# A temperature softmax whose middle loads and stores are joined in pairs

## The chip, the cores and the metric

The kernel runs on one core of a Trainium2 chip. The core has five engines with a program each: TensorE (PE), VectorE (DVE), ScalarE (ACT), GpSimd (POOL) and SyncE (SP). Data moves between the main memory (HBM) and the on-chip memory (SBUF, 128 partitions) by 16 DMA engines; SP, ACT and POOL ask for transfers, each through a queue of its own. The metric is the device time of one execution in microseconds (us). The kernel before takes 159.9 us, the median of 3 runs (159.85 to 159.92).

## The reference

The input is 16 x 1024 rows of 512 float32 numbers, 33.55 MB; the output is as large. Each row goes through a softmax at temperature 2:

```python
x_scaled = x / 2.0
x_max = np.max(x_scaled, axis=-1, keepdims=True)
exp_x = np.exp(x_scaled - x_max)
return exp_x / np.sum(exp_x, axis=-1, keepdims=True)
```

## The kernel before

The 16384 rows are spread over 128 partitions, 128 rows for each. Every partition's 128 rows are cut into ten tiles, in the order of the work: tile 0 with 3 rows, tile 1 with 5, and tiles 2 to 9 with 15 each (`TILES`, line 10; the second number is the tile's place). A row is 2048 bytes, so a 15-row tile is 30720 bytes on each partition, contiguous in HBM and in SBUF, and 3840 KB in all. The tiles lie in one SBUF tensor, `arena`, with room for 98 rows per partition: tiles 0 to 7 fill it, tile 8 lies again where tiles 0 to 2 were, and tile 9 over the rest of tile 2 and a part of tile 3.

The work of a tile is done in place:

- Its load: SP asks for tile 0, ACT for tile 1 (in three pieces, `SPREAD`) and then for tiles 2 to 7, all at the start (`early`, `loads`, line 119). POOL asks for tiles 8 and 9 later (line 177): `TURN` (83) makes it wait until the first 83 rows per partition are exponentiated, and `LATE` says which tiles' stores must have landed first (0, 1, 2 for tile 8; 3 for tile 9).
- ACT takes exp(x / 2) row by row with the row's sum into `stats` (lines 204 and 271), in chunks of 5 rows after the first 3. No maximum is subtracted; a check at the end sees to inputs for which that would not do.
- DVE takes the reciprocals of up to 15 sums (line 166) and multiplies up to 15 rows by them (line 169). For the last tile it does so in three steps of 5 rows.
- SP stores the tile once its multiplications are done (line 137), in the order of the tiles.

PE has a bookkeeping part: it waits for each tile's landing and adds the tile's number of chunks to a semaphore, from which ACT takes one for each chunk (line 194). At the end the sums are counted that lie between `LO` and `HI` (lines 180 to 196). If all do, the program ends when all stores have landed (lines 256 and 257); otherwise a second form of the computation, with the maximum, runs from line 239. In the profiled execution that second form doesn't run.

Each engine works through its own list in order; the three queues of transfers share the 16 DMA engines. A transfer over 128 partitions gives each DMA engine 8 of them, and the records of the profile have one packet per contiguous run, here one for each partition of a tile.

Of the kernel before, what the change touches and what calls it, by code (L numbers as in the profile page):

```python
# [10 lines left out]
    (3, 0), (5, 3), (15, 8), (15, 23), (15, 38), (15, 53), (15, 68), (15, 83), (15, 0), (15, 15),  # L11
]

LATE = {8: (0, 1, 2), 9: (3,)}
ARENA = 98

HEAD = [3]
# [2 lines left out]
SPREAD = 1  # L20
# [8 lines left out]
def kernel(  # L29
# [5 lines left out]
    nc = tc.nc  # L35
# [6 lines left out]
    xf = x.flatten_outer_dims()  # L42
    of = out.flatten_outer_dims()
# [16 lines left out]
    tiles, base = [], 0  # L60
# [2 lines left out]
        tiles.append((base, r, at))  # L63
        base += r

    def dram(ap, t):
        b, r, _ = tiles[t]
        return ap[b * P : (b + r) * P].rearrange("(p r) d -> p r d", r=r)

    def sb(t):  # L70
        _, r, at = tiles[t]
        return arena[:, at : at + r, :]

    straight = sum(HEAD)
# [3 lines left out]
    owner = [max(t for t, (b, _, _) in enumerate(tiles) if b <= s) for s in starts]  # L78
# [9 lines left out]
            pairs.append([k])  # L88
    upto = [1 + max(j for j, ks in enumerate(pairs) if owner[ks[0]] == t) for t in range(len(tiles))]

    ld = [nc.alloc_semaphore(f"ld{t}") for t in range(len(tiles))]
    s_home = {t: nc.alloc_semaphore(f"s_home{t}") for t in LATE}
    s_near = nc.alloc_semaphore("s_near")
    s_end = nc.alloc_semaphore("s_end")
    s_exp = nc.alloc_semaphore("s_exp")
    s_go = nc.alloc_semaphore("s_go")
    s_rec = nc.alloc_semaphore("s_rec")
    s_mul = nc.alloc_semaphore("s_mul")
# [11 lines left out]
    g_rec = nc.alloc_semaphore("g_rec")  # L110
    g_mul = nc.alloc_semaphore("g_mul")

    def load(eng, t):
        r = tiles[t][1]
        parts = [(0, P, 0, r)]
        if t == SPREAD:
            parts = [(0, P, 0, r - 1), (0, 126, r - 1, r), (126, P, r - 1, r)]
        for p, q, lo, hi in parts:
            eng.dma_start(  # L119
                out=sb(t)[p:q, lo:hi], in_=dram(xf, t)[p:q, lo:hi]  # L120
            ).then_inc(ld[t], 16)

    stored_by = {u: s_home[t] for t, us in LATE.items() for u in us}
    for t, (_, r, at) in enumerate(tiles):
        over = {u for u, (_, ru, au) in enumerate(tiles[:t]) if at < au + ru and au < at + r}
        assert over <= {u for v, us in LATE.items() if v <= t for u in us}

    def landings(ts):
        return 16 * len(list(ts))

    near = len(tiles) - 2
    sem_of = {**stored_by, near: s_near}
    at_end = landings(t for t in range(len(tiles)) if t not in sem_of)

    def store(eng, t):
        eng.wait_ge(s_mul, upto[t])
        eng.dma_start(out=dram(of, t), in_=sb(t)).then_inc(sem_of.get(t, s_end), 16)

    def take(eng, sem, n):
        eng.wait_ge(sem, n).then_inc(sem, -n)  # L140

    def rounds(eng, body):


        i = eng.alloc_register("general")
        eng.wait_ge(s_near, 16)
        eng.wait_ge(s_flag, 1)
        eng.reg_load(i, flag[0:1, 0:1])
        with eng.While(lambda: eng.snap(i, min_val=0, max_val=1) < 1):
            body()  # L150
            eng.reg_add(i, i, 1)

    def early():
        load(nc.sync, 0)
        load(nc.scalar, 1)

    def loads():
        for t in range(2, min(LATE)):
            load(nc.scalar, t)

    def program():

        for j, ks in enumerate(pairs):
            b, c = starts[ks[0]], sum(sizes[k] for k in ks)
            a = b % ARENA
            nc.vector.reciprocal(  # L166
                out=recip[:, b : b + c], in_=stats[:, b : b + c]
            )._wait_ge(s_exp, ks[-1] + 1).then_inc(s_rec, 1)
            nc.vector.tensor_mul(  # L169
                out=arena[:, a : a + c],  # L170
                in0=arena[:, a : a + c],
                in1=recip[:, b : b + c].unsqueeze(2).to_broadcast([P, c, D]),
            )._wait_ge(s_rec, j + 1).then_inc(s_mul, 1)

        nc.gpsimd.memset(ones[:, :], 1.0).then_inc(s_ones, 1)  # L175
        nc.gpsimd.wait_ge(s_exp, starts.index(TURN))
        for t, us in LATE.items():
            nc.gpsimd.wait_ge(s_home[t], landings(us))
            load(nc.gpsimd, t)
        nc.gpsimd.tensor_scalar(  # L180
            out=inside[:, :], in0=stats[:, :], scalar1=LO, scalar2=HI,
            op0=Alu.max, op1=Alu.min,
        )._wait_ge(s_exp, len(sizes)).then_inc(s_cnt, 1)
        nc.vector.scalar_tensor_tensor(  # L184
            out=inside[:, :], in0=inside[:, :], scalar=1.0, in1=stats[:, :],
            op0=Alu.mult, op1=Alu.is_equal, accum_out=count[:, :],
        )._wait_ge(s_cnt, 1).then_inc(s_cnt, 1)
        nc.vector.tensor_scalar(  # L188
            out=flag[:, :], in0=total[:, :], scalar1=float(N), scalar2=None, op0=Alu.is_ge,
        )._wait_ge(s_tot, 1).then_inc(s_flag, 1)  # L190


        for t in range(len(tiles)):
            nc.tensor.wait_ge(ld[t], 48 if t == SPREAD else 16).then_inc(s_go, owner.count(t))
        nc.tensor.wait_ge(s_ones, 1)
        nc.tensor.matmul(  # L196
            total[:, :], lhsT=count[:, :], rhs=ones[:, :], start=True, stop=True
        )._wait_ge(s_cnt, 2).then_inc(s_tot, 1)

        nc.scalar.preload_act_table(Exp)  # L200
        for k, c in enumerate(HEAD):
            take(nc.scalar, s_go, 1)
            for b in range(starts[k], starts[k] + c):
                ins = nc.scalar.activation(  # L204
                    out=arena[:, b], in_=arena[:, b], func=Exp, scale=0.5,
                    accum_out=stats[:, b : b + 1],
                )
            ins.then_inc(s_exp, 1)
        exponentials(straight, n_rows)

        for t in range(len(tiles)):
            store(nc.sync, t)

        x_g = xf.rearrange("(t p r) d -> t p r d", p=P, r=G)
        o_g = of.rearrange("(t p r) d -> t p r d", p=P, r=G)
        data = arena[:, 0:G]

        def vector():  # L220
            for i in range(n_rows // G):
                nc.vector.reduce_max(
                    out=g_max[:, :], in_=data, axis=mybir.AxisListType.X, negate=True
                )._wait_ge(g_go, i + 1).then_inc(g_top, 1)
                nc.vector.reduce_sum(
                    out=g_sum[:, :], in_=data, axis=mybir.AxisListType.X
                )._wait_ge(g_exp, i + 1).then_inc(g_add, 1)
                nc.vector.reciprocal(
                    out=g_sum[:, :], in_=g_sum[:, :]
                )._wait_ge(g_add, i + 1).then_inc(g_rec, 1)  # L230

        def scalar():
            for i in range(n_rows // G):
                nc.scalar.activation(out=data, in_=data, func=Exp, scale=0.5)._wait_ge(
                    g_sub, i + 1
                ).then_inc(g_exp, 1)

        def gpsimd():
            nc.gpsimd.wait_ge(s_end, at_end)
            for i in range(n_rows // G):  # L240
                nc.gpsimd.dma_start(out=data, in_=x_g[i]).then_inc(g_ld, 16)
                nc.gpsimd.wait_ge(g_ld, 16 * (i + 1)).then_inc(g_go, 1)
                nc.gpsimd.tensor_add(
                    out=data, in0=data, in1=g_max[:, :].unsqueeze(2).to_broadcast([P, G, D])
                )._wait_ge(g_top, i + 1).then_inc(g_sub, 1)
                nc.gpsimd.tensor_mul(
                    out=data, in0=data, in1=g_sum[:, :].unsqueeze(2).to_broadcast([P, G, D])
                )._wait_ge(g_rec, i + 1).then_inc(g_mul, 1)
                nc.gpsimd.wait_ge(g_mul, i + 1)
                nc.gpsimd.dma_start(out=o_g[i], in_=data).then_inc(g_st, 16)  # L250
                nc.gpsimd.wait_ge(g_st, 16 * (i + 1))

        rounds(nc.vector, vector)
        rounds(nc.scalar, scalar)
        rounds(nc.gpsimd, gpsimd)
        nc.sync.wait_ge(s_near, 16)
        nc.sync.wait_ge(s_end, at_end)
# [27 lines left out]
    at = next(k for k, i in enumerate(head) if type(i).__name__ == "InstDrain")  # L285
    entry.instructions = head[:at] + first + head[at:]
    act = []
    entry.instructions = list(entry.instructions) + [i for i in jumps if i not in act]
    nc.switch_body(here, parent=None, valid_engines=[i.engine for i in jumps])
    loads()  # L290
    program()


# [28 lines left out]
```

## Time and profile before

| What | Value |
|---|---|
| median of 3 runs | 159.9 us (159.85 to 159.92) |
| span of the profiled execution, first to last instruction | 158.7 us |
| difference between median and span, outside the span | 1.2 us |
| busy: ACT, DVE, POOL, PE | 80.8, 73.2, 2.2, 0.2 us |
| moved | 67.11 MB at 423 GB/s |
| packets | 3024, of which 336 under 512 bytes |
| ACT's first instruction of tiles 2, 3, 4, 5, 6, 7, 8, 9 | 17.71, 29.26, 41.77, 59.92, 78.08, 98.51, 112.74, 131.24 us |
| last store issued | 143.66 us |

The page gives no time of the profiled execution other than its span, so the span is set against the median. The slices of the page divide the span in 40 parts of 4 us each; a digit is a share in tenths. In the rows of the queues, the share is the time that a queue's packets took, of 16 engines' time in the span or in the stretch that was asked for. A queue name followed by q (SPq, ACTq) in the waits is the engine's instruction list itself. Numbers behind a transfer's row are its count, its size and the median time from its issue to its landing.

### The profile page before, as it was taken

The page shows a single profiled execution, that of the slowest core. Times are in us where ns is not written, and L with a number is a line of the kernel's source. Part 1 is how long each engine was busy: PE and PEld are TensorE (multiplying, and loading weights), DVE is VectorE, ACT ScalarE, POOL GpSimd, SP SyncE. Part 2 cuts the span into 40 slices and gives each one's busy share as a digit, 9 for nine tenths or more (in the row PEclk, how much of TensorE's full clock was granted, in tenths as well). Part 3 has the DMA queues.
Part 4 walks back from the last instruction along what each step waited for, and adds up shares of the span by engine and source line. Part 5 has one row for each costly group of instructions (what it writes and reads, how often), then busy time and mean ns, then how long its engine had stood idle before and what let it go on. Part 6 is the DMA issues. An engine that isn't in the chain of part 4 may idle for free. (4 is left out here: it accounts for less than half of the span.)

```text
span 158.7 us, 657 instructions
## 1 busy us (share of the span) xinstructions
PE 0.2 (0%) x2; PEld 0.1 (0%) x2; DVE 73.2 (46%) x27; ACT 80.8 (51%) x257; POOL 2.2 (1%) x8
## 2 busy tenths in 40 slices
PE   0000000000000000000000000000000000000000
PEld 0000000000000000000000000000000000000000
DVE  0047001992981990059500991008932981992000
ACT  0590598697498008940399001991597009940000
POOL 0000000000000000000000300000000000010000
DMA  7999998989999999999999999999999999999995
GB/s 271 382 496 396 463 437 324 480 382 485 410 457 410 457 410 449 418 449 418 441 426 441 426 434 434 426 441 426 441 418 449 418 449 410 457 403 465 403 457 256
DMA packets 3024, 67.11 MB, mean 423 GB/s; under 512 B 336, under 2 KB 336, under 8 KB 720
## 3 DMA queue, kind: packets, MB, share of 16 engines
q1 hardware_dynamic: 1584, 34.34, 50.4%
q10 hardware_dynamic: 1152, 24.90, 37.1%
q0 software_dynamic: 288, 7.86, 11.5%
HBM read 33.55 MB, written 33.55 MB: 423 GB/s over the span
## 5 line engine op out<-in xcount | busy, mean ns | idle before, releaser
L271 ACT ACTIVATE arena<-arena x125 | 76.8, 615 | 54.1 <-ACTq L140 54.1
L169 DVE TENSOR_TENSOR arena<-arena,recip 128x7680 f32<-128x7680 f32 (+2 forms) x12 | 70.2, 5847 | 0.4
L166 DVE RECIPROCAL recip<-stats 128x15 f32<-128x15 f32 (+2 forms) x12 | 2.7, 224 | 70.4 <-ACT arena L271 61.4
L271 ACT ACTIVATION_READ_ACCUMULATOR arena<-arena x125 | 23.4, 187 | 0.0
L200 ACT ACT_TABLE_LOAD x1 | 1.3, 1283 | 5.7 <-issue 5.7
L119 POOL DMA_DIRECT2D arena<-in_x_dram x2 | 1.3, 638 | 84.9 <-ACT arena L271 84.9
L204 ACT ACTIVATE arena<-arena 128x512 f32<-128x512 f32 x3 | 1.9, 619 | 0.0
L180 POOL TENSOR_SCALAR inside<-stats 128x128 f32<-128x128 f32 x1 | 0.6, 630 | 51.7 <-ACT arena L271 51.7
L204 ACT ACTIVATION_READ_ACCUMULATOR arena<-arena 128x1 f32 x3 | 0.6, 188 | 0.0
L196 PE MATMUL total<-ones,count 128*1 128x1 f32 x2 | 0.2, 164 | 143.9 <-DVE inside L184 143.9
L184 DVE SCALAR_TENSOR_TENSOR inside<-inside,stats 128x128 f32<-128x128 f32 x1 | 0.3, 282 | 0.0
L188 DVE TENSOR_SCALAR flag<-total 1x1 int32<-1x1 f32 x1 | 0.1, 146 | 0.3 <-PE total L196 0.3
L196 PEld LDWEIGHTS total<-ones,count 128*1 128x1 f32 x2 | 0.1, 80 | 143.9 <-DVE inside L184 143.9
L175 POOL MEMSET ones<- 128x1 f32 x1 | 0.1, 98 | 2.2 <-POOLq L37 2.2
L306 POOL MEMSET const-bfloat16-1.0<- 128x1 bf16 x1 | 0.1, 108 | 0.0
L306 POOL MEMSET const-uint8-127<- 128x1 uint8 x1 | 0.1, 108 | 0.0
L306 POOL MEMSET const-float32-0.0<- 128x1 f32 x1 | 0.1, 104 | 0.2 <-issue 0.2
L306 POOL MEMSET const-float32-1.0<- 128x1 f32 x1 | 0.1, 104 | 0.0
L184 DVE DVE_READ_ACCUMULATOR inside<-inside,stats 128x1 f32 x1 | 0.1, 80 | 0.0
## 6 DMA issues: line engine op xcount, KB each, us to landing
out_dram<-arena SPq DMA_DIRECT2D x8, 3840.0 KB, 26.2
arena<-in_x_dram ACTq DMA_DIRECT2D x6, 3840.0 KB, 46.7
arena<-in_x_dram POOLq DMA_DIRECT2D x2, 3840.0 KB, 33.6
out_dram<-arena SPq DMA_DIRECT2D x1, 1280.0 KB, 22.9
arena<-in_x_dram ACTq DMA_DIRECT2D x1, 1024.0 KB
arena<-in_x_dram SPq DMA_DIRECT2D x1, 768.0 KB, 5.6
out_dram<-arena SPq DMA_DIRECT2D x1, 768.0 KB, 14.6
arena<-in_x_dram ACTq DMA_DIRECT2D x1, 252.0 KB
```

The lines of the kernel that those rows point to most:

```text
L119: eng.dma_start(out=sb(t)[p:q, lo:hi], in_=dram(xf, t)[p:q, lo:hi]).then_inc(ld[t], 16)
L166: nc.vector.reciprocal(out=recip[:, b : b + c], in_=stats[:, b : b + c])._wait_ge(s_exp, ks[-1] + 1).then_inc(s_rec, 1)
L169: nc.vector.tensor_mul(out=arena[:, a : a + c], in0=arena[:, a : a + c], in1=recip[:, b : b + c].unsqueeze(2).to_broadcast([P, c, D]),)._w ...
L175: nc.gpsimd.memset(ones[:, :], 1.0).then_inc(s_ones, 1)
L180: nc.gpsimd.tensor_scalar(out=inside[:, :], in0=stats[:, :], scalar1=LO, scalar2=HI, op0=Alu.max, op1=Alu.min,)._wait_ge(s_exp, len(sizes) ...
L184: nc.vector.scalar_tensor_tensor(out=inside[:, :], in0=inside[:, :], scalar=1.0, in1=stats[:, :], op0=Alu.mult, op1=Alu.is_equal, accum_ou ...
L188: nc.vector.tensor_scalar(out=flag[:, :], in0=total[:, :], scalar1=float(N), scalar2=None, op0=Alu.is_ge,)._wait_ge(s_tot, 1).then_inc(s_f ...
L196: nc.tensor.matmul(total[:, :], lhsT=count[:, :], rhs=ones[:, :], start=True, stop=True)._wait_ge(s_cnt, 2).then_inc(s_tot, 1)
L200: nc.scalar.preload_act_table(Exp)
L204: ins = nc.scalar.activation(out=arena[:, b], in_=arena[:, b], func=Exp, scale=0.5, accum_out=stats[:, b : b + 1],)
L271: ins = nc.scalar.activation(out=data, in_=data, func=Exp, scale=0.5, accum_out=stats[:, r : n_rows - E + 1 + r][:, bass.ds(now, 1)],)
L306: nc = _bacc.Bacc("TRN2", target_bir_lowering=False, num_devices=1)
```

## The change

Six of the ten tiles are moved in pairs. A list `BLOCKS` groups the tiles: blocks 0 and 1 are tiles 0 and 1 as before, blocks 2, 3 and 4 are tiles 2 and 3, 4 and 5, 6 and 7, and blocks 5 and 6 are tiles 8 and 9 alone. (Counted from one, the joined tiles are 3 to 8.) Loads and stores, their semaphores and their waits go by block: a joined block is one load and one store of 30 rows, 61440 bytes per partition, and its rows are assigned to the partitions 30 at a time. ACT's chunks of 5 rows and DVE's multiplications of 15 stay as they are. So ACT asks for three loads of 7680 KB in place of six of 3840 KB, exponentials of a block start when the whole block has landed, and its store waits for both multiplications. POOL's load of tile 8 waits for the stores of blocks 0, 1 and 2 (with tile 3 in it), and that of tile 9 follows without a wait of its own (`LATE`).

```diff
-LATE = {8: (0, 1, 2), 9: (3,)}
+BLOCKS = [(0,), (1,), (2, 3), (4, 5), (6, 7), (8,), (9,)]
+
+LATE = {5: (0, 1, 2), 6: ()}
...
-    def dram(ap, t):
-        b, r, _ = tiles[t]
+    blocks = []
+    for ts in BLOCKS:
...
+        blocks.append((tiles[ts[0]][0], sum(tiles[t][1] for t in ts), tiles[ts[0]][2]))
...
+    def dram(ap, k):
+        b, r, _ = blocks[k]
         return ap[b * P : (b + r) * P].rearrange("(p r) d -> p r d", r=r)
...
-    near = len(tiles) - 2
+    near = len(blocks) - 2
...
-    def store(eng, t):
-        eng.wait_ge(s_mul, upto[t])
-        eng.dma_start(out=dram(of, t), in_=sb(t)).then_inc(sem_of.get(t, s_end), 16)
+    def store(eng, k):
+        eng.wait_ge(s_mul, upto[BLOCKS[k][-1]])
+        eng.dma_start(out=dram(of, k), in_=sb(k)).then_inc(sem_of.get(k, s_end), 16)
...
-        for t in range(2, min(LATE)):
-            load(nc.scalar, t)
+        for k in range(2, min(LATE)):
+            load(nc.scalar, k)
...
-        for t, us in LATE.items():
-            nc.gpsimd.wait_ge(s_home[t], landings(us))
-            load(nc.gpsimd, t)
+        for k, us in LATE.items():
+            if us:
+                nc.gpsimd.wait_ge(s_home[k], landings(us))
+            load(nc.gpsimd, k)
...
-        for t in range(len(tiles)):
-            nc.tensor.wait_ge(ld[t], 48 if t == SPREAD else 16).then_inc(s_go, owner.count(t))
+        for k, ts in enumerate(BLOCKS):
+            nc.tensor.wait_ge(ld[k], 48 if k == SPREAD else 16).then_inc(
+                s_go, sum(owner.count(t) for t in ts)
+            )
...
-        for t in range(len(tiles)):
-            store(nc.sync, t)
+        for k in range(len(blocks)):
+            store(nc.sync, k)
```

## The prediction

> **What bounds the kernel now.** Times are us from the span's start; tiles and blocks are numbered from 0 as in the code, so the joined tiles are 2 to 7 and the blocks 2, 3 and 4.
>
> First the page: busy shares, then the slices, then the queues.
>
> ```profile
> span 158.7 us, 657 instructions
> PE 0.2 (0%) x2; PEld 0.1 (0%) x2; DVE 73.2 (46%) x27; ACT 80.8 (51%) x257; POOL 2.2 (1%) x8
> ...
> DMA  7999998989999999999999999999999999999995
> ...
> q1 hardware_dynamic: 1584, 34.34, 50.4%
> q10 hardware_dynamic: 1152, 24.90, 37.1%
> q0 software_dynamic: 288, 7.86, 11.5%
> ```
>
> No engine is busy for more than 51%; the 16 DMA engines are full in every slice but the first and last, and the queues' packet times add up to 99% of the span. Transfers are the bound. q1 is SP's (tile 0's load, all stores), q10 ACT's loads, q0 POOL's loads of tiles 8 and 9. The chain of waits agrees: of the span only 6% is DVE work, at the very end, and after it SP waits for the last store:
>
> ```profile
> SPq L137 <- DVE arena L169: 137.9, 10, 20.1
> SPq L257 <- DMA out_dram<-arena: 14.7, 1, 14.7
> ```
>
> A store of 3840 KB alone takes 9.1 us (below), so of these 14.7 about 5.6 is the queue still working on tile 8's store: when tile 9 is ready at 143.66, the engines have that much work left. This cover is what the change can use up.
>
> Next, how two queues share an engine. The DMA view of 14.8 to 24, where tile 0's store (6144 bytes per partition) runs beside loads of 30720, and of 65 to 75, where both move 30720 (columns: packets, MB, share of the engines):
>
> ```profile
> q10 hardware_dynamic: 127, 3.41, 86.0%
> q1 hardware_dynamic: 128, 0.79, 20.4%
> ```
> ```profile
> q10 hardware_dynamic: 78, 2.40, 55.5%
> q1 hardware_dynamic: 78, 1.97, 45.6%
> ```
>
> 127 packets to 128, though one queue's are five times as large; 78 to 78 when most are equal. Queues take turns by packet, not by byte: a queue with larger packets gets more of the engine.
>
> Last, when the last tile's work starts and ends (ACT timeline; timelines of POOL, and of SP from 140):
>
> ```profile
> 131.24 0.63 ACT L271 ACTIVATE arena<-arena  x1 [9.20 <-ACTq L140]
> ```
> ```profile
> 87.70 1.27 POOL L119 DMA_DIRECT2D arena<-in_x_dram  x2 [84.94 <-ACT arena L271]
> ```
> ```profile
> 143.66 0.33 SPq L137 DMA_DIRECT2D out_dram<-arena  x1
> ```
>
> POOL asks for tiles 8 and 9 once the first 83 rows per partition are exponentiated (84.94 us of waiting). Tile 9's exponentials start at 131.24, its store is issued at 143.66: 12.42 us of ACT and DVE work between.
>
> **The change part by part.**
>
> *Packet cost.* q0's 256 data packets took 11.5% of 16 x 158.7 us: 1.141 us for 30720 bytes. The 128 packets of 6144 took 20.4% of 16 x 9.2: 0.235. The line through both is 0.0369 us per 1000 bytes and 0.008 fixed, so 61440 bytes cost 2 x 1.141 - 0.008 = 2.27. An engine moves 8 of the 128 partitions; three blocks, both ways, are 48 packets fewer per engine: 48 x 0.008 = 0.4 us saved, all on the bound. Bounds: 0 to 0.5 (rounding of the shares; the completion packets of six transfers are under 512 B each). I take 0.4.
>
> *Six transfers fewer (three loads on ACT, three stores on SP).* ACT issues nine loads in 5.5 us, ahead of any exponential; three fewer at 0.45 us (the median issue) let the table load and the first exponentials (6.96) come up to 1.4 earlier, and with them tile 0's store; but the engines are full of loads at that time, so nothing ends earlier: 0. On SP a store issue is 0.33 us, while it waits 137.9 us for DVE: 0. What a store costs between its neighbours: from 136 to 146, across the change from tile 7's store to tile 8's, the engines' share is 1.00 at 430 GB/s, so 0. Rival D is the other reading.
>
> *Loads of blocks 2 to 4 on ACT's queue.* ACT's exponentials wait for a whole block. Tile 2 starts at 17.71 now; block 2 has 8 x 1.14 = 9.1 us more to load and some 0.5 more of small store packets: 27.3. ACT takes 9.3 for 15 rows (29.26 to 38.6), DVE 8.5 (0.25 + 8.16 and gaps), so block 2's store is issued at 27.3 + 18.6 + 8.5 = 54.4 (tile 2's was at 35.52). Until then stores move only tiles 0 and 1, 16 small packets, while the loads run nearly alone: block 3 lands at about 48, its store is issued at 75.6. The engines are not idle: 24 packets of 2.27, 54 us, of loads are queued from the start.
>
> *Store of block 2.* A new queue's first packet comes 4 to 5 us after its issue (tile 0's store: issued 10.94, first packets about 14.9; POOL: 87.70, about 92.5): 58.4. By then block 4 has about 3.7 of 8 packets left, taken in turns with the store at 2 x 2.27: it lands at 75.4 (tile 7: about 98 now). The store has 4.3 left, alone, 9.8 us: home at 85.5. Block 3's store has been queued since 75.6, 9.4 us ahead: no gap.
>
> *POOL's gate.* It now waits for blocks 0 to 2 home (85.5) and for the first 83 rows' exponentials, which end with the first half of block 4: 75.7 + 9.3 = 85.0. It issues at 85.8, 1.9 before now; behind it on POOL is only the row count, due at the end.
>
> *Loads of tiles 8 and 9 beside stores of blocks 3 and 4.* This is the step that decides. Before, both sides moved 30720 in turns and the loads had half the engines: issue at 87.70, tile 9 in use at 131.24. Now a load packet of 1.14 takes turns with a store packet of 2.27: one third. First load packets about 91.5; block 3's store, alone from 85, has 5 packets left: 5 x 3.41 = 17.1, to 108.6; the completion packet's turn lets one load pass (1.1); block 4's 8 packets (issued 75.7 + 18.6 + 8.5 = 102.8, in time) take 8 x 3.41 = 27.3, to 137. By then 15 of the loads' 18 turns (8 data and a completion each) are done. Two data packets of tile 9 are left, 2.3 us: 139.3. The sum by bytes agrees: before, tile 8's store lands at 130.55 + 19.0 = 149.55, and with it all but the last store; take its own 9.1 off, and 0.4 saved: 140.1 for everything but two stores. Tile 8 lands after 9 turns, 91.5 + 8 x 3.41 + 1 = 120, and its store is issued at 120.3 + 9.3 + 8.5 = 138.1, first packet 139 or later: just too late to fill turns before 139.3, or in time for one, which puts 1.14 on tile 9's landing. I take half a turn: 140.7. Bounds: none, and three.
>
> *The tail.* A landing is followed by its exponentials after 0.3 (POOL's first load lands at 87.70 + 24.7 = 112.4, first exponential 112.74). Tile 9: 141.0 + 12.42 = 153.4 for the store's issue. Tile 8's store is over at about 149.2 (149.55 - 0.4): from then the engines are empty. The 5.6 us of cover are gone, and so the store's own latency shows: 9.1 of data, about 1.0 from issue to first packet (SP's first load) and 0.5 to the landing, 10.6; bounds 10.1 to 12.9 (9.1 and the 3.8 by which the first load's 5.6 exceeds its 1.8 of data). End: 153.4 + 10.6 = 164.0 against a span of 158.7: +5.3.
>
> The profiled execution's span is 158.7, the median of runs 159.9: 1.2 lie outside it, and I keep them: **165.2**.
>
> The Trainium skill, "DMA: Bandwidth & Descriptors", Queues, rings and completion order, speaks against the change: an engine drains a whole packet of some 9 to 17 descriptors from one ring before it goes on. By that a turn would be a transfer's whole part on an engine; the 127 to 128 records above, alternating in one stretch, show turns of single runs here. By whole transfers tile 9 would still come behind all of block 4, at about 140, and the end at 164 or 165.
>
> **The rivals.**
>
> *A: a 61440-byte run is served as two turns of 30720, or by bytes.* Then loads keep half of the engines. The records above show whole runs of up to 30720; none is larger, so this is open. The loads, from 91 on, are through by 91 + 18.2 x 2 = 128, before the 130.9 of now, tile 9's store is issued before 143.66, and the end is set by bytes: 159.9 - 0.4 = 159.5, or 159.9 if the fixed cost isn't saved. It decides once a load packet no longer meets a store turn over 1.5 times its own: the cover of about 4 us (149.55 - 143.66 less 1.5 of latency) then holds. This is the one that ends faster.
>
> *B: tile 8's store comes earlier among tile 9's loads.* If POOL's first packets come at 88, tile 8 lands 3 earlier and its store takes up to three turns from tile 9: 3.4 instead of 0.6, 168.0. For it: POOL issues 1.9 earlier. Against: behind larger packets its first one comes later.
>
> *C: a hole between blocks.* Block 3's store is 9.4 ahead of need, block 4's 5.8 (102.8 against 108.6). Both would have to slip past that; loads late by 8 would cost a hole of 2 on top: 167 or more.
>
> *D: each transfer has a fixed cost of its own on the engines.* By the rows at most 3.8 us (tile 0's load: 5.6 to landing, 1.8 of it data); six fewer on top of the forecast would be 22.8 less, 142.4. Against it: the share of 1.00 from 136 to 146. [...]
>
> **How the numbers follow.** The forecast (loads at a third, an empty queue before the last store) 0.71, B 0.10, A 0.09, C or larger packets slower by themselves 0.06, D 0.01; 0.03 for no measurable change by mixed effects. Range 161.5 to 168.5: the top holds B, and the forecast with the long latency (167.5); the bottom allows tile 9 three to four us earlier, if some turns are shared better than 2 to 1. A and D are left out below. The bound of what a measurement can tell is 0.2%, 0.3 us: faster 0.08 (A with its saving, D), same 0.05, slower 0.87.
>
> **What would show it.** Block 2's exponentials at about 27; in a stretch of 95 to 105, equal packets on q0 and q1 but twice the bytes on q1; POOL's issue near 86; tile 9's exponentials near 141 in place of 131.24; the last slices with a hole of 4 to 6 us; SP's wait for the last store down from 14.7 to about 10.6. Wrong it would be if q0 had half of the bytes there, or tile 9 started before 134.

## The result, and the profile after

The changed kernel takes 169.13 us (median of 7 runs, 165.84 to 172.43) against 159.87 before; the ratio of the compared runs is 1.0428, 95% interval 1.0409 to 1.0447, which is 166.7 us. It is slower, as forecast, on the far side of the forecast 165.2. Both kernels also have executions several us above their fastest (12 of 54 of the kernel before lie between 166.1 and 168.8 us, the others between 159.8 and 160.5), and the ratio compares the fast ones of both (165.84, 167.07 and 167.27 for the changed kernel). The profile below is of the changed kernel's longest execution (172.43, span 171.1); a second profile, of one that took 170.07, is shown with the experiments. No execution of it below 170 was profiled.

The page of the changed kernel, span, slices and queues:

```profile
span 171.1 us, 648 instructions
...
DMA  7999799969699979999998999988989899600298
GB/s 271 449 460 504 332 427 529 468 299 534 270 572 462 388 302 460 460 460 460 460 445 352 417 395 546 445 359 373 531 345 452 381 402 452 266 43 0 115 460 345
...
q1 hardware_dynamic: 1152, 34.34, 47.0%
q10 hardware_dynamic: 720, 24.90, 34.2%
q0 software_dynamic: 288, 7.86, 10.8%
```

The bytes are the same; the packets are fewer. What is new is the hole near the end: slices 35 to 38, from about 145 to 162, where the engines had work in every slice before. SP's waits of the changed kernel say the same from the other side:

```profile
SPq L145 <- DVE arena L177: 155.9, 7, 39.6
SPq L268 <- DMA out_dram<-arena: 10.2, 1, 10.2
```

The wait for the last store is 10.2 in place of 14.7: nothing lies ahead of that store in the queue any more. The whole loss is in where it starts. The ACT timelines (first exponentials of block 4 and of tile 9), and POOL's and SP's (the last store), of the changed kernel:

```profile
77.10 0.63 ACT L282 ACTIVATE arena<-arena  x1 [10.04 <-ACTq L148]
...
148.18 0.63 ACT L282 ACTIVATE arena<-arena  x1 [18.32 <-ACTq L148]
```
```profile
86.70 1.27 POOL L127 DMA_DIRECT2D arena<-in_x_dram  x2 [83.97 <-ACT arena L282]
```
```profile
160.59 0.33 SPq L145 DMA_DIRECT2D out_dram<-arena  x1
```

POOL asks at 86.70 instead of 87.70, yet tile 9's exponentials begin at 148.18 instead of 131.24, 16.9 later, and the last store follows 12.4 after them, as before. 16.9 later, less 4.5 of cover (14.7 - 10.2), is the 12.4 by which the span of this execution grew. That is more than the 6.8 us of the compared ratio; some of it belongs to two late DMA engines of this execution, which are looked at with the second profile. What the forecast named as the reason is in the DMA view of the changed kernel from 95 to 108 (packets, MB, share):

```profile
q1 hardware_dynamic: 63, 3.87, 69.4%
q0 software_dynamic: 55, 1.69, 30.2%
```

Nearly as many packets on both queues, but 2.3 times the bytes on the stores': the loads of tiles 8 and 9 have 30% of the engines. The kernel before, from 98 to 108, gave them nearly half:

```profile
q1 hardware_dynamic: 77, 2.37, 54.8%
q0 software_dynamic: 66, 2.03, 46.9%
```

### The profile page after: what moved, and what is told of

It reads as the page before. It is cut to its first block, busy times and chain, and to the rows that moved or that the text cites. A ratio compares the mean times of both kernels' runs of the same rounds, so it can differ in the third digit from the quotient of the medians.

```text
span 171.1 us, 648 instructions
## 1 busy us (share of the span) xinstructions
PE 0.2 (0%) x2; PEld 0.1 (0%) x2; DVE 73.2 (43%) x27; ACT 80.4 (47%) x257; POOL 2.2 (1%) x8
```

## The experiments

Three explanations were tested against each other: turns by packet with the cover used up; the long blocks as such (later exponentials, later first stores); and store packets of 61440 bytes being slower in themselves. For the first group the rows keep the changed kernel's order in HBM, and two lists say separately how tiles are joined for loads and for stores.

### Only the late stores back to single tiles

```diff
+LOADS  = [(0,), (1,), (2, 3), (4, 5), (6, 7), (8,), (9,)]
+STORES = [(0,), (1,), (2, 3), (4,), (5,), (6,), (7,), (8,), (9,)]
```

> The changed kernel, with only the stores of blocks 3 and 4 sent as two halves of 15 rows; loads and block 2's store stay joined. Theory of turns: POOL's loads of tiles 8 and 9 then meet store packets of their own size and get half of the engines, 18.2 us of data in some 36.5 from 91.5 on; tile 9's exponentials start near 128.5 in place of 141 and later, its store is issued near 141, before the queue runs empty at 149, and the time is set by bytes again: 159.6 (32 packets per engine saved at 0.008). Rival of long blocks (the later start of the first stores and the later exponentials are what costs): nothing of that is changed, so 165 to 167 as in the changed kernel. Rival of slow large packets: only 16 of 48 packet pairs go back, so two thirds of the loss stay: 163 to 165.

Measured: 160.7 us median of 10 (159.78 to 160.99), ratio 1.0044 (1.0024 to 1.0064). The profile is of the execution of 159.79. Its DMA view from 95 to 108 and ACT's first instruction of tile 9:

```profile
q0 software_dynamic: 96, 2.95, 52.5%
q1 hardware_dynamic: 106, 2.76, 49.3%
```
```profile
127.97 0.63 ACT L290 ACTIVATE arena<-arena  x1 [8.88 <-ACTq L156]
```

The loads have half of the engines again (2.95 MB to 2.76), tile 9 starts at 127.97 (128.5 expected), and 6 of the 6.8 us between 159.9 and 166.7 are gone, with block 2's exponentials as late as in the changed kernel (27.66). So the long blocks are not the cause. Some 0.8 us remain in most runs. (This kernel has fewer store packets of 61440 bytes as well, so by itself it doesn't part the turns from slow large packets; the kernels with smaller load packets below do.)

### Only the loads joined

```diff
+LOADS  = [(0,), (1,), (2, 3), (4, 5), (6, 7), (8,), (9,)]
+STORES = [(0,), (1,), (2,), (3,), (4,), (5,), (6,), (7,), (8,), (9,)]
```

> Only the loads of tiles 2 to 7 are joined, every store is of 15 rows or less. Theory of turns: no store packet is larger than a load packet, the loads on ACT's queue even get two thirds while they last, and tiles 8 and 9 get half: 159.7, not slower than before. Rival of long blocks: exponentials of block 2 still start at 27 in place of 17.7, so most of the loss stays: 163 or more. Rival of slow large packets: half of the loss, 163.

Measured: 159.92 (10 runs), ratio 1.0004 (0.9994 to 1.0014). No loss, so neither late exponentials nor large load packets cost anything. The 0.2 that three fewer loads and 24 fewer packets per engine should have saved is not seen either. The Trainium skill, "DMA: Bandwidth & Descriptors", Rules for kernel authors, advises to coalesce small transfers into large ones; at 3840 KB nothing was left to gain here.

### Only the stores joined

```diff
+LOADS  = [(0,), (1,), (2,), (3,), (4,), (5,), (6,), (7,), (8,), (9,)]
+STORES = [(0,), (1,), (2, 3), (4, 5), (6, 7), (8,), (9,)]
```

> Only the stores of tiles 2 to 7 are joined, every load is of 15 rows or less. Theory of turns: loads meet stores of twice their packet size from the first joined store on, tile 9 lands only when the stores of tiles 2 to 7 are through, near 140, and the end comes at 165 to 168 as in the changed kernel. Rival of long blocks: ACT works as early as before, 160 to 161. Rival of slow large packets: half of the loss, 163.

Measured: 162.21 (4 runs, 161.98 to 165.85), ratio 1.0143 (1.0118 to 1.0167). The theory's 165 to 168 was a miss. The turns were there, but somewhere else: ACT's own loads of tiles 6 and 7 were squeezed, so that tile 7 came into use only at 105.21, and block 4's store was issued only at 123.00 (102.8 was worked out for the changed kernel). From 112, when block 3's store was through, POOL's loads had the engines to themselves, and tile 9 landed at 123.6. SP's timeline of this kernel from 110 to 130:

```profile
123.00 0.33 SPq L153 DMA_DIRECT2D out_dram<-arena  x1
```

By the packet records 13 of the 16 engines finish tile 9's load between 121.0 and 121.6 and the other three at 123.2, while that store's first packets begin at 123.83: a hole of 2.3 to 2.8 us on most engines, which is about the size of the loss. The joined stores of blocks 2 and 3 ran beside loads of 30720 here, and their packets of 61440 took 2.28 us on average, so the loss is not that of slow large packets. Whether a squeezed load costs anything depends on which store is ready beside it.

### Tiles 6 and 7 apart

```diff
-BLOCKS = [(0,), (1,), (2, 3), (4, 5), (6, 7), (8,), (9,)]
+BLOCKS = [(0,), (1,), (2, 3), (4, 5), (6,), (7,), (8,), (9,)]
```

> The changed kernel with tiles 6 and 7 apart again, loads and stores; tiles 2 to 5 stay joined. Theory of turns: of POOL's 18 turns some 6 pass beside block 3's large store packets and the other 12 beside packets of 1.14: tile 9 lands near 135 in place of 140, its store is issued near 148, just as the queue runs empty at 149: 159.7 to 161.5, most of the loss gone though two of three pairs are still joined. Rival of long blocks or of slow large packets: two thirds of the loss stay, 163 to 165.

Measured: 168.26 (4 runs, 168.13 to 168.72), ratio 1.0537 (1.0515 to 1.0558). A clear miss: the theory of turns alone cannot give this. There is hardly a hole (a share of 0.64 from 152 to 156); the engines are busy but slow. The DMA view from 62 to 82, where block 2's and then block 3's store runs beside the load of tile 7:

```profile
DMA packets 159, 7.46 MB, mean 373 GB/s; under 512 B 0, under 2 KB 0, under 8 KB 0
...
q1 hardware_dynamic: 84, 5.16, 74.0%
q10 hardware_dynamic: 75, 2.30, 29.2%
```

A store packet takes 74.0% of 16 x 20 us over 84, 2.82 us in place of 2.27, a load packet 1.25 in place of 1.14. Summed over all packets that is 7.0 us on each engine. So the third explanation holds in part: large store packets can become slower. They need not. In the changed kernel from 60 to 74, beside loads of the same size, they kept their duration:

```profile
q10 hardware_dynamic: 48, 2.95, 48.9%
q1 hardware_dynamic: 48, 2.95, 48.6%
```

48.6% of 16 x 14 us over 48 packets is 2.27, as worked out. In the kernel with joined stores alone, beside loads of 30720, it was 2.28.

### The same with single stores, and with one joined store

```diff
-STORES = [(0,), (1,), (2, 3), (4, 5), (6,), (7,), (8,), (9,)]
+STORES = [(0,), (1,), (2,), (3,), (4,), (5,), (6,), (7,), (8,), (9,)]
```

> The kernel whose tiles 6 and 7 were apart and that took 168.3, now with every store of 15 rows or less; the loads of tiles 2 to 5 stay joined. That kernel's store packets of 61440 took up to 3 us and more in place of 2.27 from 62 on, beside loads of 30720. Theory (store packets of 61440 become slower when other engines load at the same time, those of 30720 don't): all packets back at 2.27 and 1.14, 159.8 to 160.5. Rival (it is the mixture of load sizes, 61440 and 30720, on ACT's queue that brings the engines out of step, and that costs): the slow stretch stays, 165 or more.

Measured: 159.92, ratio 1.0001 (0.9989 to 1.0013). Store packets of 30720 take 1.14 on average: with single stores the loads' mixture of sizes is harmless. With the joined stores it is not, and without the mixture the joined stores alone cost 2.3 us (162.21), so the slow stretch goes with both together.

```diff
-STORES = [(0,), (1,), (2, 3), (4, 5), (6,), (7,), (8,), (9,)]
+STORES = [(0,), (1,), (2, 3), (4,), (5,), (6,), (7,), (8,), (9,)]
```

> The kernel whose tiles 6 and 7 were apart (168.3), with the stores of block 3 halved, so that block 2's is the only store of 61440-byte packets; it runs from about 58 to 90 beside loads of 30720. Theory (large store packets become slower beside loads of 30720 once the engines are out of step): that stretch shows store packets of 2.5 to 3 again, some 3 to 4 us of engine time are lost, everything after it runs at 1.14: 162.5 to 164. Rival (the slow packets need two large stores, or come from POOL's loads): 160.

Measured: 167.09, ratio 1.0442 (1.0422 to 1.0463). The direction is right, the size was underestimated: in this kernel one joined store costs 7.1 us. Its DMA view from 62 to 82, and its share and rate (the last two columns) in four stretches:

```profile
q1 hardware_dynamic: 84, 5.16, 75.6%
q10 hardware_dynamic: 75, 2.30, 28.6%
```
```profile
62.00:82.00 20.00, 0.00 (x0) 0.00 (x0) 18.45 (x5) 14.54 (x48) 0.00 (x0) 1.00 1.04 373
90.00:97.00 7.00, 0.00 (x0) 0.00 (x0) 0.00 (x0) 4.79 (x15) 1.27 (x2) 1.00 1.04 434
97.00:105.00 8.00, 0.00 (x0) 0.00 (x0) 3.44 (x2) 4.50 (x16) 0.00 (x0) 1.00 0.94 338
105.00:115.00 10.00, 0.00 (x0) 0.00 (x0) 4.97 (x1) 0.00 (x0) 0.00 (x0) 1.00 1.02 439
```

2.88 us per store packet and 373 GB/s while the joined store runs beside loads; 434 with single stores alone; 338 once more for 8 us, when POOL's first loads come in on engines that are by now up to 3.7 us apart; 439 after that.

### Smaller load packets, no large store: the turns alone

These start from the kernel before; only POOL's two loads are sent in parts.

```diff
+        if t in LATE:
+            parts = [(0, P, 0, 5), (0, P, 5, 10), (0, P, 10, r)]
```

> The kernel before, with POOL's loads of tiles 8 and 9 each sent as three of 5 rows: 10240 bytes (0.385 us) in a packet beside store packets of 1.14. No packet is larger than before. Theory of turns with used-up cover: the loads get a quarter of the engines wherever a store is queued and catch up only while none is (about 113 to 117); tile 9 lands near 139 to 141 in place of 130.9, its store is issued near 153, after the queue ran empty at 149, and the end comes 3 to 6 us later: 163 to 166. Rival (the loss of the changed kernel is only that store packets of 61440 become slower): there are none, 160.

Measured: 169.69, ratio 1.0599 (1.0574 to 1.0625), without one packet over 30720 bytes. From 98 to 116 in the DMA view of this kernel, then ACT at tile 9 and the slices:

```profile
q1 hardware_dynamic: 202, 5.71, 73.6%
q0 software_dynamic: 208, 1.97, 25.7%
```
```profile
142.23 0.63 ACT L273 ACTIVATE arena<-arena  x1 [2.04 <-ACTq L142]
```
```profile
DMA  7989998999999989999998999899999991059988
```

Packets 202 to 208, bytes almost three to one, tile 9 at 142.23 (139 to 141 expected), and then the hole, here of 8 us since tile 8 was late as well (130.90) and its store was issued only at 148.70. The expected 163 to 166 had missed that second lateness.

```diff
+        if t in LATE:
+            parts = [(0, P, 0, 8), (0, P, 8, r)]
```

> The same with two loads of 8 and 7 rows each: a third of the engines, as in the changed kernel, but beside stores that have a pause at about 113 to 117 while tile 7 is not ready. Theory of turns with used-up cover: tile 9 lands near 134, three later than before, its store is issued near 147, still inside the cover: 159.9 to 160.5. Rival (any loss of turns shows one to one): 163.

Measured: 166.43 (4 runs, 164.88 to 175.66), ratio 1.0381 (1.026 to 1.0503). The expectation was wrong in one step: there is no pause between the stores at 113 to 117. By the packet records that is where tile 6's store runs, 108.9 to 121.6; tile 7's, issued at 115.14, had been waiting when its first packet came at 122.4. So the loads got their third all along, tile 9 started at 141.39, and the last store was issued at 153.78. With halves, with thirds and (on 14 of 16 engines) in the changed kernel tile 9 lands between 139 and 142: with any share that lets the stores of tiles 2 to 7 through first, it lands when everything else but two stores has been moved.

### The cover measured

The kernel before, with extra writes of zeros by DVE just ahead of the last reciprocal: d us of delay for the last store, and no bytes. The first kernel has one write of 2048 zeros per partition, the second three of 3584.

```diff
+            if j == len(pairs) - 1:
+                for i in range(1):
+                    ins = nc.vector.memset(pad[:, :], 0.0)
...
+                    ins.then_inc(s_pad, 1)
```

> The kernel before, with one extra DVE instruction (a write of 2048 zeros per partition into PSUM, some 2 us) just ahead of the last reciprocal and multiplication. It delays tile 9's store by its own duration d and moves no bytes. Theory of the used-up cover: the queue has work until about 149 and a new store needs some 1 us, so a store issued at 143.66 + d costs nothing while d is below 4.4: 159.9. Rival (the end follows the last store's issue one to one, as the chain of waits ends there): 159.9 + d, 162.

Measured: 159.92, ratio 0.9993 (0.998 to 1.0007). DVE's timeline has the write of 1.76 us and, with the wait around it, 2.1 us between the last two multiplications: 2.1 us later, and no cost.

The profiled execution is one that took 167.46, and its packet records show something of its own, without one packet over 30720 bytes. On one of the 16 engines 19 store packets in a row, from 48 to 98, take 1.3 to 1.7 us in place of 1.14, 7.6 us more in all. That engine finishes tile 8's store at 157.0, the others from 149.0 to 149.6, and the program ends 7.6 us later than usual. So a late engine appears without joined transfers too, and the cover does not hide it. The kernel before has executions of the same length (166.1 to 168.8); none of them was profiled.

> The same with three writes of 3584 zeros, one behind the other: d of some 6 to 12 us, to be read from the trace. Theory of the used-up cover: 159.9 + (d - 4.4), so 165 at d = 10, and a hole of d - 4.4 in the transfers before the last store. Rival: 159.9 + d, 170 at d = 10.

Measured: 165.97, ratio 1.0374 (1.0344 to 1.0404). DVE's and SP's rows of that profile:

```profile
137.99 2.83 DVE L177 TENSOR_TENSOR arena<-arena,recip 128x2560 f32<-128x2560 f32 x1
141.56 3.04 DVE L170 MEMSET pad<- 128x3584 f32 x1 [0.74 <-issue]
...
152.25 0.15 DVE L174 RECIPROCAL recip<-stats 128x5 f32<-128x5 f32 x1
```
```profile
SPq L265 <- DMA out_dram<-arena: 10.2, 1, 10.2
```

From 140.82 to 152.25, d = 11.4 in the profiled execution, which took 167.17: a cost of 7.3, so that 4.1 of the delay were covered. With the same d the median of 165.97 gives a cost of 6.1 and 5.3 covered; 4.4 were expected. The last wait is 10.2, as in the changed kernel.

### The changed kernel once more

> The changed kernel again, for a profile of an execution whose DMA engines all stay in step. Theory of turns with used-up cover: as in the first profile up to 137, tile 9's exponentials near 140.4 in place of 148.22, its store at 153, the end at 163.5 to 165, a median of 165 to 168. Where it is longer, some engines' large store packets should show durations well over 2.27. Rival (a late engine is always there and is the whole cost): exponentials of tile 9 near 148 again and an end above 170.

Measured: 169.2 (168.57 to 170.07), ratio 1.0566 (1.0512 to 1.062); the profiled execution took 170.07. ACT at tiles 8 and 9, and the engines' share in three stretches (after the clock the DMA share and GB/s):

```profile
120.72 0.63 ACT L282 ACTIVATE arena<-arena  x1 [24.94 <-ACTq L148]
145.84 0.63 ACT L282 ACTIVATE arena<-arena  x1 [15.82 <-ACTq L148]
```
```profile
138.00:144.00 6.00, 0.00 (x0) 0.00 (x0) 0.49 (x1) 0.00 (x0) 0.00 (x0) 1.00 1.02 415
144.00:152.00 8.00, 0.00 (x0) 0.00 (x0) 2.93 (x2) 6.17 (x21) 0.00 (x0) 1.00 0.66 284
153.00:159.00 6.00, 0.19 (x2) 0.09 (x2) 5.51 (x6) 2.13 (x8) 0.63 (x1) 1.00 0.00 0
```

Neither side was right on the time: the median is above the expected 165 to 168, and tile 9 starts at 145.84, not 140.4 and not 148. The hole of six us from 153 to 159 is the forecast one, but it is preceded by a stretch with a share of 0.66: some engines are done with tile 8's store while others still work. In the first profile 14 of the 16 completions of tile 9's load came from 139.4 to 139.9, where the forecast had them, and the last two at 144.8 and 147.8; in the second, ten came from 139.5 to 140.1 and six from 142.1 to 145.5. The packet records show stretched store packets on the late ones: 2.5 to 3.3 us between 91 and 135 where the others have 2.27. ACT waits for the last engine. Since a late engine appears with single transfers as well, these two profiles don't show that the joined stores brought the late ones about.

## Why the prediction was right, and what was mis-sized

- *The bound, the turns.* Right. The share of the loads is set by packet sizes: 63 packets to 55 and 69.4% to 30.2% in the changed kernel, 202 to 208 and 73.6% to 25.7% with thirds. The turns alone, with no large packet, make the kernel slower by 6.1 to 9.6 us (halves, thirds, by the ratios); halving the late stores alone brings tile 9 to 127.97. The Trainium skill, "DMA: Bandwidth & Descriptors", Queues, rings and completion order, has an engine drain a packet of several descriptors before it goes on to the next ring. The prediction's reading of it, a turn as long as a transfer's whole part on an engine, is not borne out: the 63 and 55 records above alternate by single runs, of 61440 bytes as well. How many descriptors a run has is in no record here.
- *Packet cost 2.27.* Right in the changed kernel on most engines (2.27 from 60 to 74, 2.29 from 95 to 108) and on average with joined stores alone (2.28).
- *Saving of 0.4.* Not shown: the loads' half of it gave 1.0004 (0.9994 to 1.0014).
- *Timetable.* Block 2 in use at 27.3 forecast, 27.44 measured; its store 54.4, 54.41; block 3's store 75.6, 75.56; block 4 in use 75.7, 77.10; POOL's issue 85.8, 86.70; block 4's store 102.8, 104.08; tile 8 in use 120.3, 120.57; its store 138.1, 138.37. Up to there the forecast is within 1.4 us, but the last two agree by luck. On the engines in step tile 8's load was complete at 116.7 to 117.3: the forecast added the load packet that passes at the change of stores as time, where it brings tile 8's last packet forward by a turn. Two late engines, at 120.1 and 120.2, put the landing where the forecast had it.
- *Tile 9 at 141.0.* This is the term that was mis-sized in the two profiled executions. Fourteen engines of the first and ten of the second were there by 140.1, but a tile lands with its last engine, and its exponentials began at 148.18 and 145.84. The step that came out otherwise took all 16 engines to be in step and every store packet at 2.27, a value drawn out from packets of 6144 and 30720. On the late engines single store packets took 2.5 to 3.3. The forecast had large packets that are slower by themselves as a separate case with 0.06; in these executions it came on top of the main case. Size alone is not the reason, as 2.28 with joined stores alone and the late engine with packets of 30720 show; what is stays open.
- *The tail.* Right: 12.4 from exponentials to the last store's issue (148.18 to 160.59), 10.5 from there to the end, 10.6 forecast. The cover is 4.1 by the delayed kernel's profiled execution and 5.3 by its median, 4.4 forecast.
- *Rivals.* A (two turns per packet, or by bytes) is out by the packet counts. B did not occur in the profiled executions, where tile 8's store came no earlier than 138, but only because two or more engines had tile 8 late. With all engines in step its store would be issued near 135 (117.3 + 9.3 + 8.5) and would meet the last two load packets of tile 9. At two turns of 1.14 that is 2.3 us on tile 9's 139.4, and an end near 166.2 (141.7 + 0.3 + 12.4 + 10.5 + 1.3 outside the span). That is an estimate; it lies among the times that the ratio compares (165.84 to 167.27), and none of those executions was profiled, so whether B happens in them is open. C's hole between blocks is absent here, but it is what the kernel with joined stores alone shows. D is out: three fewer loads saved nothing.

How much each part has of the 6.8 us at 166.7: the forecast mechanism gives 5.3 by its working, and the fastest run, 165.84, is 6.0 over before. The 1.5 that are left at 166.7 are not accounted for: tile 8's store among tile 9's loads and late engines are both possible. In the executions of 170.07 and 172.43 the late engines account for the further delay of tile 9. No experiment removes the stretched packets alone.

## What to carry to other kernels

When transfers bound a kernel, the packet size is also a share: a queue's part of the engines goes with the size of its packets, so joining transfers on one side takes bandwidth from the other side just then. Look for the load that the last tile waits for, and for what is in the queue behind which that wait hides; here some 4 to 5 us of stores were the whole cover. Joining loads that were already 3840 KB gained nothing measurable, and joining stores of that size cost 1.4% even with single loads. Where 16 engines share a tile, look at all its completions: one late engine holds up the tile.

## What the runs showed of the hardware that was not expected

- In two kernels whose loads on ACT's queue mix 61440 and 30720 bytes, store packets of 61440 took 2.82 and 2.88 us on average from 62 to 82. They took 2.27 beside loads of 61440 from 60 to 74 in the changed kernel, 2.29 beside POOL's loads of 30720 from 95 to 108 (69.4% of 16 x 13 us over 63), and 2.28 on average with joined stores alone, where every load is of 30720 or less. So neither the store's size nor the size of the load beside it is enough. With the joined stores alone, the packet records from 54 to 70 have stores of 2.5 to 2.9 on three engines out of step with the others, and 2.27 on those in step. That being out of step is the cause was not tested.
- One joined store out of nine is enough for 7.1 us in such a kernel. By the packet records 5.4 of the 6.4 us per engine that its kernel's packets took over their usual duration lie between 60 and 100, while it runs and as the next loads begin.
- Store packets of 30720 can be stretched as well: in the profile of the kernel with one extra write, on one engine, 19 of them took 1.3 to 1.7 us beside loads of 1.14, and that alone was 7.6 us. In the profile of the kernel before, from 60 to 74, all 16 engines stood within 0.6 us of one another and every packet of 30720 took 1.14 to 1.15.
